# Where the sums of weight blocks are made in the seven-product groups of a decoder trunk

## The chip, the cores and the metric

The kernel runs on one NeuronCore of a Trainium2 chip. The core has a matrix engine (TensorE, PE in the profile, with its weight loads as PEld), a vector engine (VectorE, DVE), a scalar engine (ScalarE, ACT), a general engine (GpSimd, POOL), and a queue engine (SyncE, SP) that here only issues transfers. Sixteen DMA engines move data between HBM and SBUF (the on-chip memory) for all queues. TensorE writes its results to PSUM. The metric is the device time of one execution in microseconds (us); lower is better.

## What is computed

Two layers of a decoder trunk on 256 tokens of width 2048, then a final RMSNorm. Per layer:

```python
h = rms_norm(x, norm_w)
proj = h @ w_in                       # split into qa, ka, va, za, qi, ki, wi, ub, zb, qc, kc, vc, zc, gates
y_a = (dsa_attention(...) * silu(za)) @ w_a_out
y_b = (conformer_conv(ub, ...) * silu(zb)) @ w_b_out
y_c = (stick_breaking_attention(qc, kc, vc) * silu(zc)) @ w_c_out
g = sigmoid(gates).reshape(b, s, 3, 2048)
merged = g[:, :, 0] * y_a + g[:, :, 1] * y_b + g[:, :, 2] * y_c
x = x + merged @ w_out
```

All of it is float32. The change lies in the second half of a layer: the merge gates (`gates`, 6144 columns of `w_in`), the three branch projections, and `w_out`.

## The kernel before

**Split weights.** Each float32 weight unit (256 rows by 512 columns, 512 KB, held as 128x1024) is turned into two halves of a faster format: ScalarE rounds it (`high`, L247, tile `wh`), VectorE takes the rest (`low`, L251, tile `wl`, = raw minus `wh`). Three matmuls stand for one product: activation high by `wh`, activation low by `wh`, activation high by `wl`, in this order. `wh` and `wl` have three buffers each.

**Steps.** The second half of a layer is a list of steps (`Step`), run by `run` (L551). A plain step (`plain`) takes one unit for both token tiles: 12 matmuls of 512 columns. `run` works ahead: at step s it issues raw loads up to step s+7 (`PARTS` + `LOADS`), does the early events of s, converts the unit of step s+2 (`high`, `low`), then emits the matmuls of step s and its late events. Raw loads go to SP's queue, into a ring of five `raw` buffers and one buffer `va` that attention also uses (`raw_unit`, L406).

**Groups of seven products.** `Seven` (L446) computes one block of 256 tokens by 1024 columns over half of the inner dimension with seven half-size products instead of eight (M1 to M7). Each product has two half steps, a and b, of 6 matmuls. Weight blocks are called here B00, B01, B10, B11 (row half, column half). M1, M2 and M3 use B00, B10 and B11 as they are loaded. The others use sums:

| product | block sum | where it is kept |
|---|---|---|
| M5 | B01 + B00 | `ar` (`homes[h]`) |
| M6 | B01 + B00 + B11 | `ar` |
| M4 | B01 + B00 + B11 + B10 | `ar` |
| M7 | B01 + B11 | `ph` and `pl` (`third[h]`) |

Before the change they are made thus, for each half: `two` loads B01 into `ar` (SP queue); `plus` adds the raw B00 of M1 on VectorE (L473); `more` adds B11 with an accumulating DMA from GpSimd's queue (L470), after M5 has been converted; `plus` adds the raw B10 of M2 on VectorE; `three` loads B01 again into `ph` or `pl` (L478), and `and_more` adds B11 with a second accumulating DMA (L481). There are five groups per layer (four for gates, one for `w_out`), ten in all, so twenty halves. `ph` and `pl` are also working tiles of attention (`pair`).

**Order.** `gather` weaves the half steps of a group with plain steps (`y`: other chunks or branch projections; `c`, `d`: the rest of the group's own columns over the other half of the inner dimension). Per layer: a gate chunk, a branch-A projection, group g2, a projection, group h2, the 16 steps `zb`, group g1, group h1, two projections, then the `w_out` steps `qs` with group `o`. In the background VectorE works off the taps of a depthwise convolution (L678) and its normalisation (`conv_norm`), started by `norm` at an offset from the first step of `zb`; and attention's last part (`stick`) ends while g2 begins. Every branch result is turned by a way over DRAM (`turned`: transposes on VectorE, transfers L294 and L300 on GpSimd's queue).

**Queues.** Every engine runs its instructions in order. A scheduler orders them when the program is built, from priorities and its own estimate of time; a transfer without a tie to another instruction may be put well ahead of where it is written. `issue_after(ins)` ties an instruction behind `ins` on the same queue; `high_priority` moves instructions ahead.

Of the kernel before, what the change touches and what calls it, by code (L numbers as in the profile page):

```python
# [11 lines left out]
ALU = mybir.AluOpType  # L12
AX = mybir.AxisListType

P = 128
# [13 lines left out]
PARTS = 2  # L29
LOADS = 5  # L30
LATER = 10
# [20 lines left out]
def trunk(ctx: ExitStack, tc: tile.TileContext, x, w_in, xt, w_a, w_b, w_c, w_out,  # L52
          fnw, consts, out):
    nc = tc.nc
# [14 lines left out]
    def issue_after(ins):  # L69
        return nullcontext() if fixed[0] else tc.issue_after(ins)  # L70
# [45 lines left out]
    class Lazy(list):  # L116
        def __init__(self, n, make):
            super().__init__([None] * n)
            self.make = make
# [182 lines left out]
    def turned(srcs, use, later=LATER, tmp=None):  # L302


        n = len(srcs)
        if tmp is None:
            tmp = tp.tile([P, n * 512], F32, tag="zt", bufs=1, name=nm("zt"))
        c = srcs[0].shape[1]
        z = away([v.rearrange("p (k e) -> p k e", e=P) for v in srcs], tmp[:, :n * c])

        def rest():
            y = tp.tile([P, n * 512], F32, tag="zy", bufs=1, name=nm("zy"))
            y = y[:, :n * c].rearrange("p (u k i) -> p u k i", u=n * 4, i=32)
            back(z, y)
            yield later - 2
            yield from use(y)

        pending.append([count[0] + 2, rest()])
# [78 lines left out]
    def source(w, k0, kn, c0, n=512):  # L397
        return w[k0 * P:(k0 + kn) * P, c0:c0 + n].rearrange("(k p) c -> p k c", p=P)
# [3 lines left out]
        return [v[:, i] for i in range(2)]  # L402

    ring = [0]

    def raw_unit(w, k0, c0):  # L406
        ring[0] += 1
        if ring[0] % (RAWS + 1):
            raw = wp.tile([P, 2, 512], F32, tag="raw", bufs=RAWS, name=nm("raw"))
        else:  # L410
            raw = sp.tile([P, 2, 512], F32, tag="va", bufs=1, name=nm("va"))
        nc.sync.dma_start(raw, source(w, k0, 2, c0))
        return raw

    def plain(w, k0, c0, act, banks, start, stop, nk=2):
# [30 lines left out]
    class Seven:  # L446


        def __init__(self, w, c0, act, sums, added=("P1", "P4")):
            self.banks = banks = {}  # L450
            self.steps = {}

# [7 lines left out]
            def block(k, n, h):  # L460
                return source(w, k * 4 + h * 2, 2, c0 + n * 512)

            homes = [ar[:, h * 1024:(h + 1) * 1024].rearrange("p (k c) -> p k c", k=2) for h in range(2)]
            third = {}

            def two(h):
                nc.sync.dma_start(homes[h], block(0, 1, h))

            def more(h, k, n):
                nc.gpsimd.dma_start(homes[h], block(k, n, h), accum_op=ALU.add)  # L470

            def plus(h, name):
                nc.vector.tensor_add(homes[h], homes[h], self.steps[name, h].raw)  # L473

            def three(h):
                g = ("ph", "pl")[h]
                third[h] = tp.tile([P, 1024], F32, tag=g, bufs=1, name=nm(g)).rearrange("p (k c) -> p k c", k=2)
                nc.sync.dma_start(third[h], block(0, 1, h))  # L478

            def and_more(h):  # L480
                nc.gpsimd.dma_start(third[h], block(1, 1, h), accum_op=ALU.add)  # L481

            def product(name, a, k0, t, to, start, load, late=False):
                for h in range(2):
# [18 lines left out]
            product("M4", act, 4, 1, "Y", False, lambda h: homes[h], True)  # L503
            st = self.steps
            for h in range(2):
                st["M5", h].at(-PARTS - 9, partial(two, h), True)
                if "P1" in added:
                    st["M1", h].at(-PARTS + 1, partial(plus, h, "M1"), True)
                else:
                    st["M5", h].at(-PARTS - 5, partial(more, h, 0, 0), True)  # L510
                st["M5", h].at(-PARTS + 1, partial(more, h, 1, 1), True)
                if "P4" in added:
                    st["M2", h].at(-PARTS + 1, partial(plus, h, "M2"), True)
                else:
                    st["M6", h].at(-PARTS + 1, partial(more, h, 1, 0), True)
                st["M7", h].at(-PARTS - 8, partial(three, h), True)
                st["M7", h].at(-PARTS - 4, partial(and_more, h), True)
            held = once(ev)

            def copied(n, get):  # L520
# [183 lines left out]
    xn = next_x()  # L704
# [9 lines left out]
    for layer in range(DEPTH):  # L714
        w = w_in[layer]
# [699 lines left out]
        def emit_x(xc, accs, q, c0, ts):  # L1415
            n = xc.shape[-1]
            with tc.high_priority(offset=URGENT):
                for a_, t in zip(accs, ts):
                    nc.vector.tensor_add(xc[:, t, :], a_, xc[:, t, :])  # L1419
            if last:  # L1420
                sq = ev()
                for t in ts:
                    with tc.high_priority(offset=URGENT):
                        nc.scalar.activation(sq[:, :n], xc[:, t, :], AF.Square, accum_out=ssq[:, t, q:q + 1])  # L1424
                    nc.vector.tensor_mul(xfr[t][:, c0:c0 + n], xc[:, t, :], fwl[0][:, c0:c0 + n])
            else:
                x_squares([xc[:, t, :] for t in ts], ssq, q, ts)
                turned([xc[:, t, :] for t in ts], partial(x_parts_F, xn, c0 // P, nwn), LATER - (2, 2, 3, 4)[q],
                       t4() if q % 2 else None)

        def store_x(xc, c0):
# [53 lines left out]
            steps[-1].at(1, finished).at(-4, ask)  # L1485
            return steps

        def gates(b, j, added=("P1", "P4")):
            c0 = O_G + b * D + j * 512
            g = Seven(w, c0, hx, sums, added)  # L1490
            rest = [[plain(w, k0, c0 + i * 512, hx, lambda i=i: [g.bank(v) for v in ("XY", "ZW")[i]], False, k0 == KD - 2)
                     for k0 in range(KC, KD, 2)] for i in range(2)]
            for i in range(2):
                rest[i][-1].at(1, lambda i=i: keep_gate(b, j + i, [g.bank(v) for v in ("XY", "ZW")[i]]))
            return g, rest[0], rest[1]
# [21 lines left out]
            for ks in ((0, 1), (2, 3)):  # L1517
                differences([x8[:, i * 4 + ks[0]:i * 4 + ks[0] + 2, :] for i in range(2)], osums, ks)

        g2, c2, d2 = gates(2, 0)  # L1520
        h2, e2, f2 = gates(2, 2)
        g1, c1, d1 = gates(1, 0)
        h1, e1, f1 = gates(1, 2)
        y2, y1 = ([products(b, wy, j, gx) for j in range(4)] for b, wy, gx in ((2, wc, gc), (1, wb, gb)))
        zb = gate_steps(O_ZB, cv, gb, lambda: bool(stages))
        zb[0].at(-16, norm)
        y1[3][0].at(0, output_sums)
        if last:
            y1[3][1].at(0, lambda: nc.sync.dma_start(fwl[0], fnw.partition_broadcast(P)))
        o = Seven(wo, p0 * 512, mx, osums)  # L1530
        qs = {}
        for q in range(4):
            own = q in (p0, p0 + 1)
            banks = (lambda v: lambda: [o.bank(n) for n in v])("ZW" if q - p0 else "XY") if own else None
            qs[q] = output(q, banks, KC if own else 0)
        begin = "g.M1a y g.M5a y g.M1b y g.M5b y g.M6a y g.M6b y g.M2a y g.M2b y g.M7a g.M7b "
        rest = "g.M3a g.M3b d g.M4a d g.M4b c d c d c*2"
        steps = chunk_steps(w, O_G + 2 * 512, hx, KD, partial(keep_gate, 0, 2)) + products(0, w_a[layer], 2, ga)
        steps += gather(begin + rest, y=chunk_steps(w, O_G + 3 * 512, hx, KD, partial(keep_gate, 0, 3), wide_accs), g=g2, c=c2, d=d2)
# [5 lines left out]
        steps += y1[2] + y1[3]  # L1545
        c, d = 2 - p0, 3 - p0
        if last:
            steps += qs[c][:4] + qs[d] + gather(
                "g.M1a c g.M5a g.M1b c g.M5b g.M6a c g.M6b c g.M2a g.M2b g.M7 g.M3a g.M3b f g.M4a f g.M4b f*2 e*4",
                g=o, c=qs[c][4:], e=qs[p0], f=qs[p0 + 1])  # L1550
        else:
            steps += qs[c][:4] + qs[d][:4] + gather(
                "g.M1a c g.M5a c g.M1b d g.M5b d g.M6a c g.M6b c g.M2a d g.M2b d g.M7 g.M3a g.M3b e g.M4a e g.M4b e*2 f*4",
                g=o, c=qs[c][4:], d=qs[d][4:], e=qs[p0], f=qs[p0 + 1])
        extra = []
        if not last:
# [1 line left out]
        order = ExitStack()  # L1558
        pass
        pass  # L1560
        early_parts = run(steps, extra)
        fixed[0] = False
        order.close()
# [114 lines left out]
```

## Time and profile before

| | |
|---|---|
| time, median of 3 runs (lowest, highest) | 2024.99 us (2024.75, 2026.19) |
| the profiled execution's own time | 2028.66 us |
| its span in the trace | 2026.9 us |
| granted TensorE clock, mean | 0.997 |
| VectorE busy | 1671.6 us |
| ScalarE busy | 1140.9 us |
| GpSimd busy (issuing transfers) | 219.6 us |
| moved by DMA | 482.68 MB |

The page sums the busy time of each engine over one profiled execution; the views of its trace list waits by who waited for whom, groups of instructions, single stretches, and transfers with their time from issue to landing. An entry in square brackets on a line of the timeline is the idle time of that engine just before the instruction, and what ended it.

### The profile page before, as it was taken

How to read it: one execution, taken by the hardware profiler on the slowest of the kernel's cores; microseconds unless marked ns; L12 is line 12 of the kernel's file. 1: busy time of each engine (PE TensorE's matmuls, PEld its weight loads, DVE VectorE, ACT ScalarE, POOL GpSimd, SP SyncE). 2: the span in 40 equal slices, each digit the busy share in tenths (PEclk: the TensorE clock that was granted, in tenths of full speed). 3: DMA queues.
4: the chain of work that ended last, by engine and by line, in shares of the span. 5: the costliest groups of instructions: out<-in, count | busy, mean ns of one | idle time of the engine just before them, and what ended most of it. 6: DMA issues, size and time to landing. Idle time of an engine off the chain costs nothing. (4 is left out here: it accounts for less than half of the span.)

```text
span 2026.9 us, 25983 instructions
## 1 busy us (share of the span) xinstructions
PE 1996.2 (98%) x9266; PEld 1664.7 (82%) x9266; DVE 1671.6 (82%) x2227; ACT 1140.9 (56%) x1327; POOL 219.6 (11%) x324
## 2 busy tenths in 40 slices
PE   9999999999999999999999999999999999999998
PEld 8899888888878787878888988888888787878776
DVE  8667899878988979777885779988879989697777
ACT  7556555565655556555654555455666555565545
POOL 0111112100110001011110111121001000010110
PEclk9999999999999999999999999999999999999999
DMA  7798679855787777897877876788657888678974
GB/s 273 231 287 263 186 225 296 258 177 177 218 227 247 212 249 223 255 317 241 301 227 237 283 240 192 237 283 254 180 177 223 223 259 256 209 226 237 345 237 136
DMA packets 245378, 482.68 MB, mean 238 GB/s; under 512 B 17856, under 2 KB 30656, under 8 KB 245120
## 3 DMA queue, kind: packets, MB, share of 16 engines
q1 hardware_dynamic: 214208, 399.74, 61.8%
q0 software_dynamic: 29376, 78.14, 15.0%
q10 hardware_dynamic: 1664, 3.15, 0.4%
q8 instruction: 72, 1.18, 0.2%
q14 instruction: 58, 0.48, 0.1%
HBM read 448.18 MB, written 32.77 MB: 237 GB/s over the span
## 5 line engine op out<-in xcount | busy, mean ns | idle before, releaser
L262 PE MATMUL acc<-wh,s 128*128 128x512 f32 (+1 forms) x4528 | 1136.2, 390 | 14.1 <-ACT wh L247 11.4
L247 ACT CAST wh<-raw 128x1024 fp32r<-128x1024 f32 (+1 forms) x650 | 678.7, 1047 | 612.2 <-PE acc L262 430.1
L262 PEld LDWEIGHTS acc<-wh,s 128*128 128x128 f32 x4528 | 843.8, 188 | 183.6 <-ACT wh L247 14.3
L251 DVE TENSOR_TENSOR wl<-raw,wh 128x1024 fp32r<-128x1024 f32 (+1 forms) x651 | 787.1, 1213 | 196.0 <-ACT wh L247 193.5
L262 PE MATMUL acc<-wl,s 128*128 128x512 f32 (+1 forms) x2072 | 565.2, 389 | 3.5 <-DVE wl L251 2.9
L262 PEld LDWEIGHTS acc<-wl,s 128*128 128x128 f32 x2072 | 387.2, 188 | 88.7 <-DVE wl L251 11.4
L262 PE MATMUL mm<-wh,s 128*128 128x512 f32 x992 | 246.6, 390 | 2.4 <-DVE s L615 1.2
L262 PEld LDWEIGHTS mm<-wh,s 128*128 128x128 f32 x992 | 185.9, 188 | 42.6 <-ACT wh L247 1.6
L294 POOL DMA_DIRECT2D z<-zt x192 | 112.7, 603 | 953.5 <-DVE zt L291 935.6
L678 DVE SCALAR_TENSOR_TENSOR s<-yT,cst,s 128x256 f32<-128x256 f32 x480 | 212.2, 477 | 0.0
L262 PE MATMUL mm<-wl,s 128*128 128x512 f32 x496 | 133.0, 390 | 1.0 <-DVE wl L251 1.0
L247 ACT CAST wh<-ar 128x1024 fp32r<-128x1024 f32 x60 | 63.0, 1050 | 85.6 <-DMA ar<-in_w_in_dram 35.9
L262 PEld LDWEIGHTS mm<-wl,s 128*128 128x128 f32 x496 | 92.8, 188 | 21.5 <-DVE wl L251 2.4
L251 DVE TENSOR_TENSOR wl<-ar,wh 128x1024 fp32r<-128x1024 f32 x60 | 73.1, 1219 | 41.2 <-ACT wh L247 40.4
L247 ACT CAST wh<-va 128x1024 fp32r<-128x1024 f32 x52 | 54.5, 1049 | 45.7 <-PE acc L262 24.6
L251 DVE TENSOR_TENSOR wl<-va,wh 128x1024 fp32r<-128x1024 f32 x52 | 63.3, 1218 | 13.4 <-ACT wh L247 13.2
L473 DVE TENSOR_TENSOR ar<-ar,raw 128x1024 f32<-128x1024 f32 x37 | 45.0, 1219 | 34.0 <-DMA raw<-in_w_in_dram 24.4
L262 PEld LDWEIGHTS mm<-s,wl 128*128 128x128 f32 x512 | 66.9, 191 | 5.0
L300 POOL DMA_DIRECT2D zy<-z x50 | 37.0, 740 | 287.4 <-DMA z<-zt 96.0
L262 PE MATMUL mm<-s,wl 128*128 128x192 f32 x512 | 66.0, 271 | 0.0
L291 DVE STREAM_TRANSPOSE zt<-acc 128x512 f32<-128x512 f32 (+1 forms) x68 | 45.2, 679 | 3.5 <-PE acc L262 3.0
L470 POOL DMA_DIRECT2D ar<-in_w_in_dram x16 | 19.3, 1203 | 194.3 <-DVE wl L251 194.3
(273 smaller groups left out, 1226.9 us busy)
## 6 DMA issues: line engine op xcount, KB each, us to landing
raw<-in_w_in_dram SPq DMA_DIRECT2D x507, 512.0 KB, 4.5
raw<-in_w_out_dram SPq DMA_DIRECT2D x51, 512.0 KB, 5.4
zy<-z POOLq DMA_DIRECT2D x48, 512.0 KB, 5.5
z<-zt POOLq DMA_DIRECT2D x184, 128.0 KB, 4.5
raw<-in_w_a_dram SPq DMA_DIRECT2D x29, 512.0 KB, 4.2
va<-in_w_in_dram SPq DMA_DIRECT2D x28, 512.0 KB, 4.7
raw<-in_w_c_dram SPq DMA_DIRECT2D x26, 512.0 KB, 5.0
raw<-in_w_b_dram SPq DMA_DIRECT2D x26, 512.0 KB, 6.8
```

What stands on the lines that cost most here:

```text
L247: newest_parts[0] = nc.scalar.copy(u[1], u[0])
L251: newest_parts[1] = sub = nc.vector.tensor_sub(u[2], u[0], u[1].bitcast(F32))
L262: newest[0] = nc.tensor.matmul(o, lhsT, rhs, start=start, stop=stop, skip_group_check=True)
L291: nc.vector.transpose(tmp[:, t].rearrange("p b k i -> p k b i"), src.rearrange("p k (b c) -> p k b c", b=4, c=32))
L294: nc.gpsimd.dma_start(z[:, :, :, a, :].rearrange("t b c e -> c (t b) e"), tmp[a * 32:(a + 1) * 32].rearrange("c t b k i -> c (t b) (k i)"))
L300: nc.gpsimd.dma_start(y.rearrange("p (t a) k i -> p t (a k i)", a=4), z.rearrange("t b c a e -> (b c) t (a e)"))
L470: nc.gpsimd.dma_start(homes[h], block(k, n, h), accum_op=ALU.add)
L473: nc.vector.tensor_add(homes[h], homes[h], self.steps[name, h].raw)
L678: nc.vector.scalar_tensor_tensor(o, yT[:, c, q:q + S], wq, o, op0=ALU.mult, op1=ALU.add)
```

## The change

Four things are changed.

1. `three` loads B11, not B01, and `and_more` and the `more` of B11 are not used any more. VectorE makes all sums: `first_sums` (third += `ar`, giving B01 + B11, then `ar` += raw of M1, giving B01 + B00), `second_sum` (`ar` = third + raw of M1, giving B01 + B00 + B11), `last_sum` (`ar` += raw of M2). All are issued with high priority. A half thus has four VectorE additions and two plain loads, where it had two additions, two plain loads and two accumulating DMAs.
2. The loads `two` and `three` are tied behind the newest raw load in SP's queue, and stand `lead` and `lead` + 1 steps ahead of M5's conversion (7 and 8, for the first group 5 and 6); before, `two` stood 9 ahead of it and `three` 8 ahead of M7's.
3. The weaving: one plain step moves from between M5a and M1b to between M7a and M7b. In the last layer the four steps of the chunk `d` are woven into group `o` and no longer stand ahead of it.
4. `norm` starts 22 steps ahead of `zb`, not 16; the transposed parts of x are used one step earlier in two of four chunks (`LATER`); the ring of raw buffers starts anew in each layer.

```diff
     class Seven:
-        def __init__(self, w, c0, act, sums, added=("P1", "P4")):
+        def __init__(self, w, c0, act, sums, lead=7, added=("P4",)):
...
             def two(h):
-                nc.sync.dma_start(homes[h], block(0, 1, h))
+                with issue_after(last_raw[0].ins):
+                    nc.sync.dma_start(homes[h], block(0, 1, h))
...
-            def plus(h, name):
-                nc.vector.tensor_add(homes[h], homes[h], self.steps[name, h].raw)
...
-                nc.sync.dma_start(third[h], block(0, 1, h))
-
-            def and_more(h):
-                nc.gpsimd.dma_start(third[h], block(1, 1, h), accum_op=ALU.add)
+                with issue_after(last_raw[0].ins):
+                    nc.sync.dma_start(third[h], block(1, 1, h))
+
+            def first_sums(h):
+                with tc.high_priority():
+                    nc.vector.tensor_add(third[h], third[h], homes[h])
+                    nc.vector.tensor_add(homes[h], homes[h], self.steps["M1", h].raw)
+
+            def second_sum(h):
+                with tc.high_priority():
+                    nc.vector.tensor_add(homes[h], third[h], self.steps["M1", h].raw)
+
+            def last_sum(h):
+                with tc.high_priority():
+                    nc.vector.tensor_add(homes[h], homes[h], self.steps["M2", h].raw)
...
             for h in range(2):
-                st["M5", h].at(-PARTS - 9, partial(two, h), True)
-                if "P1" in added:
-                    st["M1", h].at(-PARTS + 1, partial(plus, h, "M1"), True)
-                else:
-                    st["M5", h].at(-PARTS - 5, partial(more, h, 0, 0), True)
-                st["M5", h].at(-PARTS + 1, partial(more, h, 1, 1), True)
+                st["M5", h].at(-PARTS - lead, partial(two, h), True)
+                st["M1", h].at(-PARTS, partial(first_sums, h), True)
+                st["M5", h].at(-PARTS + 1, partial(second_sum, h), True)
                 if "P4" in added:
-                    st["M2", h].at(-PARTS + 1, partial(plus, h, "M2"), True)
+                    st["M2", h].at(-PARTS + 2, partial(last_sum, h), True)
                 else:
                     st["M6", h].at(-PARTS + 1, partial(more, h, 1, 0), True)
-                st["M7", h].at(-PARTS - 8, partial(three, h), True)
-                st["M7", h].at(-PARTS - 4, partial(and_more, h), True)
+                st["M5", h].at(-PARTS - lead - 1, partial(three, h), True)
...
-        zb[0].at(-16, norm)
+        zb[0].at(-22, norm)
...
-        begin = "g.M1a y g.M5a y g.M1b y g.M5b y g.M6a y g.M6b y g.M2a y g.M2b y g.M7a g.M7b "
+        begin = "g.M1a y g.M5a g.M1b y g.M5b y g.M6a y g.M6b y g.M2a y g.M2b y g.M7a y g.M7b "
         rest = "g.M3a g.M3b d g.M4a d g.M4b c d c d c*2"
...
         if last:
-            steps += qs[c][:4] + qs[d] + gather(
-                "g.M1a c g.M5a g.M1b c g.M5b g.M6a c g.M6b c g.M2a g.M2b g.M7 g.M3a g.M3b f g.M4a f g.M4b f*2 e*4",
-                g=o, c=qs[c][4:], e=qs[p0], f=qs[p0 + 1])
+            steps += qs[c][:4] + gather(
+                "g.M1a d g.M5a g.M1b d g.M5b d g.M6a d g.M6b c g.M2a c g.M2b c g.M7a c g.M7b g.M3a g.M3b f g.M4a f g.M4b f*2 e*4",
+                g=o, c=qs[c][4:], d=qs[d], e=qs[p0], f=qs[p0 + 1])
         else:
             steps += qs[c][:4] + qs[d][:4] + gather(
-                "g.M1a c g.M5a c g.M1b d g.M5b d g.M6a c g.M6b c g.M2a d g.M2b d g.M7 g.M3a g.M3b e g.M4a e g.M4b e*2 f*4",
+                "g.M1a c g.M5a g.M1b c g.M5b d g.M6a d g.M6b c g.M2a c g.M2b d g.M7a d g.M7b g.M3a g.M3b e g.M4a e g.M4b e*2 f*4",
```

More of the change, by code (lines that the diff above doesn't have):

```diff
@@ L404, in trunk @@
     ring = [0]
+    last_raw = [None]
     def raw_unit(w, k0, c0):
@@ L411, in raw_unit @@
             raw = sp.tile([P, 2, 512], F32, tag="va", bufs=1, name=nm("va"))
-        nc.sync.dma_start(raw, source(w, k0, 2, c0))
+        last_raw[0] = nc.sync.dma_start(raw, source(w, k0, 2, c0))
         return raw
@@ L1427, in emit_x @@
                 x_squares([xc[:, t, :] for t in ts], ssq, q, ts)
-                turned([xc[:, t, :] for t in ts], partial(x_parts_F, xn, c0 // P, nwn), LATER - (2, 2, 3, 4)[q],
+                turned([xc[:, t, :] for t in ts], partial(x_parts_F, xn, c0 // P, nwn), LATER - (2, 2, 4, 5)[q],
                        t4() if q % 2 else None)
@@ L1486, in output, with gates @@
             return steps
-        def gates(b, j, added=("P1", "P4")):
+        def gates(b, j, lead=7):
             c0 = O_G + b * D + j * 512
-            g = Seven(w, c0, hx, sums, added)
+            g = Seven(w, c0, hx, sums, lead)
             rest = [[plain(w, k0, c0 + i * 512, hx, lambda i=i: [g.bank(v) for v in ("XY", "ZW")[i]], False, k0 == KD - 2)
@@ L1518, in output_sums @@
                 differences([x8[:, i * 4 + ks[0]:i * 4 + ks[0] + 2, :] for i in range(2)], osums, ks)
-        g2, c2, d2 = gates(2, 0)
+        g2, c2, d2 = gates(2, 0, 5)
         h2, e2, f2 = gates(2, 2)
@@ L1529, in trunk @@
             y1[3][1].at(0, lambda: nc.sync.dma_start(fwl[0], fnw.partition_broadcast(P)))
-        o = Seven(wo, p0 * 512, mx, osums)
+        o = Seven(wo, p0 * 512, mx, osums, added=("P4",))
         qs = {}
@@ L1560, in trunk @@
         pass
+        ring[0] = 0
         early_parts = run(steps, extra)
```

## The prediction

> **What bounds the kernel now.** I read the page first, then the list of waits of TensorE, then the timeline at each wait, then transfers, then VectorE by stretches.
>
> ```profile
> PE 1996.2 (98%) x9266; PEld 1664.7 (82%) x9266; DVE 1671.6 (82%) x2227; ACT 1140.9 (56%) x1327; POOL 219.6 (11%) x324
> ```
>
> TensorE is the bound, busy for all but 30.7 us of the span of 2026.9. Its pace, in a stretch without waits:
>
> ```profile
> 1601.61 1.77 PEld L262 LDWEIGHTS mm<-wh,s 128*128 128x128 f32 x8
> ```
>
> Eight weight loads start within 1.77 us less the 0.19 us of one, so a matmul of 512 columns starts every (1.77 - 0.19) / 7 = 0.226 us. A plain step of 12 is 2.71 us, a half step of 6 is 1.36 us. The change alters neither number nor size of the matmuls; it can only touch the waits, listed here from 10 us on (who waited for whom, us in total, times, longest):
>
> ```profile
> PE acc L262 <- ACT wh L247: 11.4, 7, 2.6
> PE acc L262 <- DVE wl L251: 2.9, 8, 1.1
> PE acc L262 <- ACT acc L522: 2.7, 1, 2.7
> PE mm L262 <- DVE s L615: 1.2, 1, 1.2
> PE mm L262 <- ACT wh L247: 1.0, 1, 1.0
> PE mm L262 <- DVE wl L251: 1.0, 2, 0.6
> PE mm L262 <- ACT s L614: 0.3, 1, 0.3
> ```
>
> That is 20.5 us. The timeline of TensorE places the large ones (the idle time stands in brackets):
>
> ```profile
> 608.45 2.08 PE L262 MATMUL acc<-wh,s 128*128 128x512 f32 x4 [2.62 <-ACT wh L247]
> ...
> 891.29 3.68 PE L262 MATMUL acc<-wh,s 128*128 128x512 f32 x8 [2.10 <-ACT wh L247]
> ...
> 1037.90 0.50 PE L262 MATMUL acc<-wh,s 128*128 128x512 f32 x1 [0.28 <-ACT wh L247]
> ...
> 1782.71 0.50 PE L262 MATMUL acc<-wl,s 128*128 128x512 f32 x1 [1.15 <-DVE wl L251]
> ...
> 1800.71 1.21 PE L262 MATMUL mm<-wl,s 128*128 128x512 f32 x4 [0.62 <-DVE wl L251]
> ...
> 1895.23 2.11 PE L262 MATMUL acc<-wh,s 128*128 128x512 f32 x8 [1.76 <-ACT wh L247]
> ```
>
> Of the first row's seven waits, 11.4 us, those at 891 and 1895 make 3.9 and that at 1037 makes 0.3; the other four, 7.2 us, lie at 608, 793, 1609 and 1796 us, each in front of a half of M6 in a gate group. The 2.7 us behind L522 lie at 1964 us, in front of M6 of the last layer's group `o`.
>
> ScalarE is only the messenger. Its own timeline just before:
>
> ```profile
> 607.36 1.04 ACT L247 CAST wh<-ar 128x1024 fp32r<-128x1024 f32 x1 [5.81 <-DMA ar<-in_w_in_dram]
> ...
> 889.25 1.04 ACT L614 CAST s<-zy 128x1024 fp32r<-128x1024 f32 x1 [6.67 <-DMA zy<-z]
> ...
> 1962.55 1.04 ACT L247 CAST wh<-ar 128x1024 fp32r<-128x1024 f32 x1 [5.91 <-DMA ar<-in_w_out_dram]
> ```
>
> At 607 and 1962 the conversion of M6 waits for the accumulating DMA into `ar`; the casts ahead of the three waits between read `ar` for M6 likewise. At 889 (and alike before 1895) ScalarE stands in front of a cast whose transposed branch result is late, with the next weight conversion queued behind it. Why transfers are late, by issue to landing (median us last):
>
> ```profile
> raw<-in_w_in_dram SPq DMA_DIRECT2D x507, 512.0 KB, 4.5
> ```
> ```profile
> ar<-in_w_in_dram POOLq DMA_DIRECT2D x16, 512.0 KB, 8.6
> ```
>
> An accumulating transfer takes twice a plain one, and M6's can be issued only once M5 is converted.
>
> **The change, part by part.** *Accumulating DMAs out.* Forty transfers of 512 KB go. The five waits for them, 7.2 + 2.7 = 9.9 us, go with them: the sum behind M5 becomes one VectorE addition. What is late next there is that addition, below. After two of the long waits, at 608 and at 891, TensorE ran on a lower clock:
>
> ```profile
> 605.00:615.00 10.00, 7.38 (x27) 5.70 (x26) 6.57 (x8) 5.04 (x5) 0.00 (x0) 0.83 0.39 118
> 687.00:719.00 32.00, 31.30 (x136) 24.91 (x135) 32.00 (x39) 16.55 (x17) 2.38 (x2) 1.00 0.91 271
> 719.00:763.00 44.00, 44.00 (x197) 36.47 (x196) 31.81 (x30) 22.74 (x26) 3.11 (x5) 1.00 0.74 230
> 763.00:825.00 62.00, 60.33 (x263) 48.70 (x263) 58.33 (x66) 39.12 (x44) 7.91 (x9) 1.00 0.83 238
> 890.00:900.00 10.00, 8.71 (x31) 7.12 (x32) 7.14 (x6) 7.16 (x9) 0.72 (x1) 0.83 1.04 361
> ```
>
> (Stretch, busy of PE, PEld, DVE, ACT, POOL, clock, DMA share, GB/s.) In the first and the last stretch the clock is 0.83, so 10 x 0.17 = 1.7 us were lost in each besides the wait. The first goes too: 1.7. The Trainium skill ("TensorE: Matmul & The Clock Gate", Part 1: The HAM clock gate) says that the clock halves after at least one idle window of about 3.4 us. By that, waits of 2.62 and 2.10 us would cost no clock, and -16 would become -13; the trace disagrees, and I go by it.
>
> *Loads tied to their place.* Group `o` of layer 0 converts its first sum at 946 us, yet its loads stand from 869 us on, together with accumulations, and the transposed result's own transfer is issued between them:
>
> ```profile
> 946.68 1.05 ACT L247 CAST wh<-ar 128x1024 fp32r<-128x1024 f32 x1 [1.67 <-PE mm L262]
> ```
> ```profile
> 869.36 0.37 SPq L478 DMA_DIRECT2D ph<-in_w_out_dram  x1
> ```
> ```profile
> 877.12 1.22 POOL L481 DMA_DIRECT2D ph<-in_w_out_dram  x1 [8.42 <-DMA ph<-in_w_out_dram]
> 877.87 1.22 POOL L300 DMA_DIRECT2D zy<-z  x1
> ```
>
> That transfer lands at 889, 11 us later. With the tie, these loads move some 50 us later, and the accumulations do not exist. The waits of 2.10 and 1.76 us and the clock after the first go: 5.6 us. The moved issues pass the raw loads between on SP's queue; they wait only for `ar`, `ph` and `pl`, free since the group before.
>
> *Start of `norm`, and the last layer's order.* At 1782.71 and 1800.71 VectorE is behind; its queue holds the end of `conv_norm` there. Six steps earlier, about 13 us of it fall into the `zb` steps, where VectorE has room (719 to 763 above: 31.81 busy of 44). Those two waits go, 1.15 + 0.62 = 1.8 us. The wait of 1.2 us for L615 is for the last transposed part in the last layer; its reader stands about 4 us later in the new order, and the cast before it no longer queues behind the accumulation: 1.2 us. *Ring and `LATER`*: nothing; a load is issued five steps ahead of its conversion either way, and if one were a step late it would cost up to 2.7 us.
>
> *Weaving.* As many steps as before. Where M7a, M7b, M3a and M3b stood in a row, 5.4 us of TensorE for four conversions of 1.22, three half steps stand now; M5a and M1b, apart before, stand together. Only short waits lie there (the 2.9 us on `wl` less 1.15 at 1782 fall on seven places), so I count nothing for it, within the 1.8 us of these.
>
> *VectorE's additions in.* One costs 1.22 us:
>
> ```profile
> L473 DVE TENSOR_TENSOR ar<-ar,raw x37: 1178/1222/1228, 576.8 to 1970.6; 128x1024 f32<-128x1024 f32 x37
> ```
> ```profile
> 576.78 2.35 DVE L473 TENSOR_TENSOR ar<-ar,raw 128x1024 f32<-128x1024 f32 x2
> ```
>
> Twice two halves in ten groups make 40 more, 48.8 us, 4.9 us per group. They lie beside the matmuls as long as the conversions are in time. The tightest step is the plain one after M1a: `second_sum` of half a and `first_sums` of half b, three additions, stand in front of M1b's conversion. From M1a's start at 0: M5a is converted at 1.0 + 1.2 = 2.2 (cast, then rest); three additions, 2.35 - 1.22 = 1.13 each back to back, end at 5.6; M1b's `wl` at 6.7. TensorE starts M1b at 1.36 + 2.71 + 1.36 = 5.4 and needs `wl` after four matmuls, at 6.3: 0.4 us late, in ten groups 4.0 us. Bounds: 0 if the scheduler puts the conversion first; 1.2 us more per group if VectorE comes to that step one instruction late, 16 us. I take 4.0, nearest to the row. In the stretch 687 to 719 VectorE has no idle time; there it can only shift taps and normalisation into `zb`, whose 44 us have 12 idle. In 763 to 825 it has 3.7 idle plus what `norm` gives up.
>
> Holding M1's raw block three steps longer costs nothing: its buffer is asked for again six loads later, M2a's, five steps ahead of need. In g2, `third` is tied to attention's end, as its load was before; nothing, bounds -1 and +3 us per layer.
>
> **Sum**: 9.9 + 1.7 + 5.6 + 1.8 + 1.2 = 20.2 us go, 4.0 come: -16 us. The profiled execution took 2028.66 us with a span of 2026.9; its own time would become 2012. The median of the runs shown is 2024.99, so the median becomes 2009.
>
> **The rivals.**
>
> *All of it, and free* (0.17). The additions find gaps, and other small waits on VectorE go as well: the 20.5 us of waits and 3.4 of clock vanish: 2001. For: VectorE is 18% idle. Against: not where groups stand.
>
> *VectorE full* (0.16). In g2, h2 and g1 of both layers the additions displace conversions: of 6 x 4.9 = 29 us half lands on TensorE, 14.6 in place of 4, net -5.5: 2019. For: 32.00 of 32 busy. Against: most of the rest there is background work.
>
> *VectorE held at the head of its queue: slower* (0.10). `first_sums` waits for two loads and a raw block, and all conversions stand behind it. Such waits exist:
>
> ```profile
> DVE ar L473 <- DMA raw<-in_w_in_dram: 24.4, 9, 3.9
> ```
>
> A conversion between plain steps has slack: two steps and eight matmuls, 7.2 us, less 1.04 for the cast and 1.22 (as L473) for the rest, so 4.9 us. Waits of 24.4 / 9 = 2.7 us cost nothing. It decides from 4.9 us on: were the tied loads as late as an accumulation, 9 us instead of 4.5, a wait would be near 7.5 us and cost 2.6, in 20 halves 52 us on paper; with only the first half of each group in plain steps, 26. Net +10: 2035. Against: without accumulations the loads should land in 5.
>
> *Waits only move* (0.07): the tied loads are now what M5 and M7 wait for, as much as before: 2025.
>
> *VectorE holds up GpSimd* (0.02). Two-input additions could delay GpSimd's issuing of the transposed results: 1.2 us each at the two late ones per layer, 5 us back: 2014. Against:
>
> ```profile
> L470 POOL DMA_DIRECT2D ar<-in_w_in_dram x16: 1179/1198/1267, 588.9 to 1851.4; - x16
> ```
>
> The spread is 0.09 us with VectorE over 80% busy, so nothing holds it. The Trainium skill ("SBUF — State Buffer", SBUF: two separate sides) describes such a lock on a shared port, for two SBUF inputs only against a GpSimd operation that reads SBUF; no run here shows it.
>
> **How the numbers follow.** Forecast 2009 (0.48). Range: from 1999, the free case with g2's -1 us in both layers, to 2022, which holds the half-full VectorE and the bound of 16 us for the additions (2021); beyond lie the slower and the unchanged case, 0.17. A change under 0.2%, 4 us, cannot be told from none. Faster: forecast, free, shared port and most of the full case, 0.80; same 0.10; slower 0.10.
>
> **What would show it.** Right: no accumulating transfer in the list of issues; no cast of `wh` from `ar` idle for a DMA; no loads of `o` before 900 us; no clock of 0.83 past 20 us; additions 80 by 1.22 us. Wrong: waits of TensorE on `wl` above 7 us in total (VectorE full), or VectorE idle for `ph`, `pl` or `ar` loads over 5 us at once (held).

## The result and the profile after

| | before | after |
|---|---|---|
| time, median of 5 runs (lowest, highest) | 2024.99 us (2023.88, 2027.38) | 2014.38 us (2012.42, 2016.85) |
| profiled execution, and its span | 2028.66, 2026.9 | 2015.98, 2014.1 |

The ratio is 0.9947, with an interval of 0.9932 to 0.9961: 10.6 us faster, where 16 were forecast. From here on TensorE's idle time counts past the first 10 us; the start is the same in all kernels.

The page of after, its busy times and its transfers:

```profile
PE 1991.2 (99%) x9266; PEld 1667.6 (83%) x9266; DVE 1715.3 (85%) x2267; ACT 1142.7 (57%) x1327; POOL 171.2 (9%) x284
...
DMA packets 234498, 461.70 MB, mean 229 GB/s; under 512 B 17216, under 2 KB 30016, under 8 KB 234240
```

The change does what it says: forty transfers of 512 KB are gone (482.68 - 461.70 = 21.0 MB), and VectorE has 40 instructions and 43.7 us more. The waits of TensorE in after (who waited for whom, us in total, times, longest):

```profile
PE mm L262 <- ACT s L620: 4.2, 1, 4.2
PE acc L262 <- DVE wl L251: 3.1, 4, 1.8
PE acc L262 <- ACT wh L247: 2.5, 4, 1.0
PE mm L262 <- ACT wh L247: 2.4, 2, 1.3
...
PE mm L262 <- DVE wl L251: 0.5, 1, 0.5
```

That is 12.7 us instead of 20.5. The row left out belongs to the start. All the large waits of before are gone, at 608, 793, 891, 1609, 1796, 1895 and 1964 us, and so are the two at 1782 and 1800. In their place stand others. The timeline of TensorE in after:

```profile
590.93 1.45 PE L262 MATMUL acc<-wh,s 128*128 128x512 f32 x5 [1.00 <-ACT wh L247]
...
772.93 1.07 PE L262 MATMUL acc<-wh,s 128*128 128x512 f32 x4
774.73 0.73 PE L262 MATMUL acc<-wl,s 128*128 128x512 f32 x2 [0.73 <-DVE wl L251]
775.29 2.00 PE L262 MATMUL mm<-wh,s 128*128 128x512 f32 x8
...
1770.25 0.74 PE L262 MATMUL acc<-wl,s 128*128 128x512 f32 x2 [0.45 <-DVE wl L251]
...
1926.06 0.73 PE L262 MATMUL acc<-wl,s 128*128 128x512 f32 x2 [1.79 <-DVE wl L251]
...
1957.04 2.07 PE L262 MATMUL mm<-wh,s 128*128 128x512 f32 x4 [4.24 <-ACT s L620]
```

Four kinds are to be seen. **M1b**: at 774 and 1770 M1b waits for `wl` after its four matmuls with `wh`, 1.18 us in all. In the second layer the same half step of the same group waited in before too, 1.15 us at 1782; there only 0.45 are left. **M5a of the last `o`**: at 1926 TensorE waits 1.79 us for the `wl` that is made from `ar`. **The first group, g2**: at 590.93 (and for 0.95 us at 1586) M5a waits for its cast. **The last branch**: at 1957 TensorE waits 4.24 us for a turned result, and the weight casts have nothing to do with it.

The rows at 773 also show what a wait costs beyond its bracket. Four matmuls at 0.226 us make the next one due at 773.83; it came at 774.73, 0.90 late, where the bracket says 0.73. The one behind the two `wl` matmuls was due at 775.18 and came at 775.29. So this wait took 0.28 us more than its bracket; the sums below take that for each.

What VectorE did ahead of 590.93, and ScalarE's cast of M5a:

```profile
583.96 1.22 DVE L482 TENSOR_TENSOR ph<-ph,ar 128x1024 f32<-128x1024 f32 x1
585.10 1.22 DVE L251 TENSOR_TENSOR wl<-raw,wh 128x1024 fp32r<-128x1024 f32 x1
586.23 1.22 DVE L482 TENSOR_TENSOR pl<-pl,ar 128x1024 f32<-128x1024 f32 x1
587.36 1.22 DVE L251 TENSOR_TENSOR wl<-raw,wh 128x1024 fp32r<-128x1024 f32 x1
588.50 2.36 DVE L483 TENSOR_TENSOR ar<-ar,raw 128x1024 f32<-128x1024 f32 x2
```
```profile
589.83 1.04 ACT L247 CAST wh<-ar 128x1024 fp32r<-128x1024 f32 x1 [4.19 <-DVE ar L483]
```

The addition that M5a needs, the first of L483, is placed behind the `pl` sum of the other half, which is not needed before that half's sum for M6b.

The chain behind 1957, and ahead of it the `wl` of M5a that ends the wait at 1926, in the timelines of VectorE, GpSimd and ScalarE of after (L1386 and L1387 merge a branch result, L291 transposes it, L300 brings it back from DRAM):

```profile
1920.17 1.23 DVE L482 TENSOR_TENSOR pl<-pl,ar 128x1024 f32<-128x1024 f32 x1 [0.58 <-DMA ar<-in_w_out_dram]
...
1924.79 1.21 DVE L251 TENSOR_TENSOR wl<-ar,wh 128x1024 fp32r<-128x1024 f32 x1
...
1926.52 1.21 DVE L487 TENSOR_TENSOR ar<-ph,raw 128x1024 f32<-128x1024 f32 x1
...
1931.06 0.68 DVE L1387 TENSOR_TENSOR s<-s,t 128x512 f32<-128x512 f32 x1
1931.66 1.21 DVE L487 TENSOR_TENSOR ar<-pl,raw 128x1024 f32<-128x1024 f32 x1
...
1936.40 1.22 DVE L491 TENSOR_TENSOR ar<-ar,raw 128x1024 f32<-128x1024 f32 x1
...
1939.81 0.70 DVE L291 STREAM_TRANSPOSE zt<-s 128x512 f32<-128x512 f32 x1
```
```profile
1948.25 0.72 POOL L300 DMA_DIRECT2D zy<-z  x1 [5.11 <-ACT wh L247]
```
```profile
1955.94 1.04 ACT L620 CAST s<-zy 128x1024 fp32r<-128x1024 f32 x1 [3.87 <-DMA zy<-z]
```

The merge ends at 1931.7, but the transpose of the second token tile comes 8 us later, behind additions and conversions (the first tile's ran at 1923.06). In before both transposes ran from 1932.89 on, in one piece; what held the part up there came later, when its transfer back waited 13.47 us, in the end for L615, which was still reading the part before it out of the one buffer `zy`:

```profile
1932.89 1.29 DVE L291 STREAM_TRANSPOSE zt<-s 128x512 f32<-128x512 f32 x2
```
```profile
1950.28 0.72 POOL L300 DMA_DIRECT2D zy<-z  x1 [13.47 <-DVE s L615]
```

### The profile page after: what moved, and what is told of

Read it like the earlier page. It is cut to its first block, busy times and chain, and to the rows that moved or that the text cites. A ratio compares the mean times of both kernels' runs of the same rounds, so it can differ in the third digit from the quotient of the medians.

```text
span 2014.1 us, 25976 instructions
## 1 busy us (share of the span) xinstructions
PE 1991.2 (99%) x9266; PEld 1667.6 (83%) x9266; DVE 1715.3 (85%) x2267; ACT 1142.7 (57%) x1327; POOL 171.2 (9%) x284
## 2 busy tenths in 40 slices
DMA packets 234498, 461.70 MB, mean 229 GB/s; under 512 B 17216, under 2 KB 30016, under 8 KB 234240
## 3 DMA queue, kind: packets, MB, share of 16 engines
q8 instruction: 72, 1.18, 0.2%
## 4 chain that ended last, share of the span: by engine, by line
PE 94%; DMA 2%; DVE 2%; issue 1%; ACT 0%; POOL 0%; DVEq 0%; SPq 0%; POOLq 0%; ACTq 0%
PE acc L262 74%; PE mm L262 17%; DMA ar<-in_w_out_dram 1%; DVE wl L251 1%; DMA va<-in_w_a_dram 1%; PE mm L1099 1%; PE mm L1189 0%; DMA zy<-z 0%; DVE ar L483 0%; PE mm L1292 0%; PE mm L1157 0%; PE mm L1239 0%; ACT wh L247 0%; DMA z<-zt 0%; PE mm L866 0%
## 5 line engine op out<-in xcount | busy, mean ns | idle before, releaser
L262 PEld LDWEIGHTS mm<-wl,s 128*128 128x128 f32 x496 | 93.6, 189 | 20.5 <-DVE wl L251 0.9
L300 POOL DMA_DIRECT2D zy<-z x50 | 35.9, 719 | 298.3 <-DMA z<-zt 104.5
L291 DVE STREAM_TRANSPOSE zt<-acc 128x512 f32<-128x512 f32 (+1 forms) x68 | 45.4, 681 | 3.6 <-PE acc L262 3.0
L620 ACT CAST s<-zy 128x1024 fp32r<-128x1024 f32 x20 | 20.9, 1046 | 13.6 <-DVE zy L670 9.8
L621 DVE TENSOR_TENSOR s<-zy,s 128x1024 fp32r<-128x1024 f32 x20 | 24.4, 1221 | 3.7 <-ACT s L620 3.7
```

Source lines behind the costliest of these rows:

```text
L262: newest[0] = nc.tensor.matmul(o, lhsT, rhs, start=start, stop=stop, skip_group_check=True)
L291: nc.vector.transpose(tmp[:, t].rearrange("p b k i -> p k b i"), src.rearrange("p k (b c) -> p k b c", b=4, c=32))
L300: nc.gpsimd.dma_start(y.rearrange("p (t a) k i -> p t (a k i)", a=4), z.rearrange("t b c a e -> (b c) t (a e)"))
L620: nc.scalar.copy(h, src)
L621: nc.vector.tensor_sub(l, src, h.bitcast(F32))
```

## The experiments

Each experiment ran beside the kernel before, in one of three sessions and in four to twelve runs; ratios are to the before of the same session, with intervals of 95%.

| kernel | median us | ratio (interval) |
|---|---|---|
| after | 2014.38 | 0.9947 (0.9932 to 0.9961) |
| e3 before + sums on VectorE only | 2007.82 | 0.9922 (0.9904 to 0.9941) |
| e4 before + ties only | 2043.77 | 1.0099 (1.0082 to 1.0117) |
| e7 after, additions left out | 1997.87 | 0.9859 (0.9844 to 0.9875) |
| e6 after + 20 more VectorE operations | 2022.91 | 0.9981 (0.9968 to 0.9993) |
| e1 after, last merge and transposes first | 2006.54 | 0.9915 (0.9899 to 0.9932) |
| e2 after, old order of the last layer | 2014.04 | 0.9950 (0.9933 to 0.9966) |
| e8 after without ties | 2007.08 | 0.9907 (0.9892 to 0.9922) |
| e14 after, `o` alone without ties | 2004.62 | 0.9895 (0.9882 to 0.9909) |
| e15 e14, M5a's sum first in g2 | 2002.86 | 0.9888 (0.9874 to 0.9902) |
| e13 e8, norm's small operations and M5a's sum first | 2007.47 | 0.9910 (0.9896 to 0.9924) |
| e9 e3, `norm` at -22 | 2006.50 | 0.9902 (0.9887 to 0.9918) |
| e5 after, `norm` at -16 | 2013.29 | 0.9941 (0.9927 to 0.9955) |

### The sums alone, and the ties alone

e3 takes over the sums, with their loads at the new places in the list of steps, and leaves weaving, `norm`, `LATER` and the ring as they were, without ties (as a diff from after):

```diff
-                with issue_after(last_raw[0].ins):
-                    nc.sync.dma_start(homes[h], block(0, 1, h))
+                nc.sync.dma_start(homes[h], block(0, 1, h))
...
-                with issue_after(last_raw[0].ins):
-                    nc.sync.dma_start(third[h], block(1, 1, h))
+                nc.sync.dma_start(third[h], block(1, 1, h))
...
-        zb[0].at(-22, norm)
+        zb[0].at(-16, norm)
...
```

> The kernel before with the sums on VectorE alone: four additions per half and no accumulating transfers, loads at their new offsets but not tied to the raw loads; old weaving, old start of the normalisation, old use of the transposed parts, old ring. By the prediction's terms this has the 9.9 + 1.7 us of the accumulation waits less 4.0 us for the additions, so 2025 - 7.6 = 2017. If most of the gain hangs on the ties and the weaving, it stays within 3 us of 2025. If the ties and the weaving are worth nothing by themselves, it is at 2014 like the changed kernel, or below, as the last layer's old order has no wait of 4.2 us.

e4 is before with the two ties:

```diff
...
-                nc.sync.dma_start(homes[h], block(0, 1, h))
+                with issue_after(last_raw[0].ins):
+                    nc.sync.dma_start(homes[h], block(0, 1, h))
...
-                nc.sync.dma_start(third[h], block(0, 1, h))
+                with issue_after(last_raw[0].ins):
+                    nc.sync.dma_start(third[h], block(0, 1, h))
```

> The kernel before with one edit: the plain loads of the block sums (into ar, ph and pl) are tied behind the newest raw load in SP's queue; the accumulating transfers stay. By the prediction the burst of group o's loads near 870 to 890 us and near 1880 us goes, with the waits of 2.1 and 1.8 us and the low clock after the first: 5.6 us, so 2019. The rival (the burst was late because of the accumulations in it, not because it stood early): no more than 1 us, 2024.

The sums alone gain more than the whole change: 2007.82, the last of the outcomes named for them, in which the ties and the weaving are worth nothing by themselves. The two intervals overlap a little, but the slowest run of e3 (2011.57) was faster than the fastest of after (2012.42). The ties alone lose 18 us, which neither expectation had. The waits of TensorE in e4, and two casts of M6 on ScalarE:

```profile
PE acc L262 <- ACT wh L247: 18.8, 7, 6.5
PE acc L262 <- ACT acc L525: 12.2, 1, 12.2
```
```profile
609.11 1.04 ACT L247 CAST wh<-ar 128x1024 fp32r<-128x1024 f32 x1 [11.11 <-DMA ar<-in_w_in_dram]
...
1979.55 1.04 ACT L247 CAST wh<-ar 128x1024 fp32r<-128x1024 f32 x1 [15.40 <-DMA ar<-in_w_out_dram]
```

The waits at 891 and 1895 are gone, as expected of the tie, but those for accumulations grew from 9.9 to some 30 us, and the mean granted clock fell from 0.997 to 0.990. GpSimd's timeline in e4 shows why:

```profile
1963.51 1.23 POOL L484 DMA_DIRECT2D ph<-in_w_out_dram  x1 [4.99 <-DMA ph<-in_w_out_dram]
1968.08 1.21 POOL L484 DMA_DIRECT2D pl<-in_w_out_dram  x1 [3.34 <-DMA pl<-in_w_out_dram]
1968.82 2.90 POOL L472 DMA_DIRECT2D ar<-in_w_out_dram  x2
```

GpSimd now has to wait for the later loads of `ph` and `pl`, and M6's accumulations into `ar` stand behind them in its queue; in before, they were issued at 1953.15 and 1958.34 (by then TensorE stands some 7.5 us later in e4). e3 has no tie, and neither wait (891, 1895). So either is enough: with the tie the burst at `o` goes even with its accumulations, and without accumulations it does no harm in its early place.

### What the additions cost

e7 leaves the 80 additions out, so that it computes less; loads, casts and matmuls stay:

```diff
             def first_sums(h):
-                with tc.high_priority():
-                    nc.vector.tensor_add(third[h], third[h], homes[h])
-                    nc.vector.tensor_add(homes[h], homes[h], self.steps["M1", h].raw)
+                pass
...
```

> The changed kernel without any addition of block sums: M4 to M7 use single blocks in place of the sums, so this leaves out part of the computation; loads, conversions and matmuls are all there. It prices the 80 additions. Prediction: they cost 4.0 us, plus whatever displaced work costs; with the 6.6 us near 1957 us now known to come from displaced merges, the time is 2004. If the additions were wholly hidden but for that wait, 2008. If VectorE is full, 2000 or less.

e6 adds one operation of the same size to each half:

```diff
                     nc.vector.tensor_add(homes[h], third[h], self.steps["M1", h].raw)
+                    nc.vector.tensor_tensor(homes[h], homes[h], homes[h], op=ALU.max)
```

> The changed kernel with one more VectorE operation of the same size per half, on the block sum right behind second_sum (the maximum of the sum with itself, which changes no value): 20 operations of 1.22 us in all, 24 us of VectorE. If an addition costs what the prediction took, 4.0 us for 40, about 2 us more: 2016. If VectorE is full around the groups, most of it lands on TensorE: 2025 to 2035. If additions are free, 2014.

All waits of TensorE that are left in e7, the start's among them:

```profile
PE mm L262 <- ACT wh L247: 1.3, 2, 0.7
PE mm L862 <- DVE eps L79: 1.1, 1, 1.1
PE acc L262 <- ACT wh L247: 0.5, 2, 0.3
```

So the 80 additions cost after 2014.38 - 1997.87 = 16.5 us (17.8 by the ratios), and without them 27 us of before are gone. Of the outcomes named for e7 this is the one for a full VectorE, 2000 or less. Forty of the 80 stood in before too, so the 16.5 bounds the price of the 40 new ones from above; but the waits at 590, 774, 1586, 1926 and 1957, most of it, are not in before. Both numbers fit the waits. From e7 to after, idle time grows from 1.8 to 12.7, 10.9; eight more waits at 0.28 make 2.2; and low clock at 1957 (below) makes 3.0: 16.1. In e6, twenty operations more cost 8.5 us (6.9 by the ratios), 0.43 each: a third of their 1.22 us lands on TensorE, though VectorE was 15% idle. That lies between the 2016 and the 2025 named beforehand. Not all of it is a full queue: two of e6's new waits, 1.51 and 1.44 us at 601 and 1600, are for M6a's cast, directly behind the added operation.

### The wait at 1957

e1 moves the merge and the transposes ahead of the additions:

```diff
-            merge(b, j, y, [sg[:, t, :] for t in range(NT)])
-            if b == 1:
-                turned([mg(j, t) for t in range(NT)], partial(use_m, j), LATER - 3 * (j == 3))
+            with tc.high_priority(offset=URGENT) if last and b == 1 and j == 3 else nullcontext():
+                merge(b, j, y, [sg[:, t, :] for t in range(NT)])
+                if b == 1:
+                    turned([mg(j, t) for t in range(NT)], partial(use_m, j), LATER - 3 * (j == 3))
```

> The changed kernel, with one edit in the last layer: the gated merge and the transposes of the last quarter of branch B (j = 3) are given the highest priority, ahead of the additions of group o. In the changed kernel TensorE waits 4.2 us near 1957 us for the split of the last transposed part and then runs at half pace for some 2.4 us. Theory A (the new additions push the merge and the second transpose back on VectorE, from 1933 us to 1940 us, and so the part arrives late): the wait goes, the clock stays up, and the time falls by 5 to 7 us, to 2008 us. Theory B (the transposed part is late because its own transfers over DRAM are slow among the raw loads): the transposes come earlier, but the wait stays above 3 us and the time stays within 2 us of 2014.

e2 gives the last layer its old weaving:

```diff
-            steps += qs[c][:4] + gather(
-                "g.M1a d g.M5a g.M1b d g.M5b d g.M6a d g.M6b c g.M2a c g.M2b c g.M7a c g.M7b g.M3a g.M3b f g.M4a f g.M4b f*2 e*4",
-                g=o, c=qs[c][4:], d=qs[d], e=qs[p0], f=qs[p0 + 1])
+            steps += qs[c][:4] + qs[d] + gather(
+                "g.M1a c g.M5a g.M1b c g.M5b g.M6a c g.M6b c g.M2a g.M2b g.M7 g.M3a g.M3b f g.M4a f g.M4b f*2 e*4",
+                g=o, c=qs[c][4:], e=qs[p0], f=qs[p0 + 1])
```

> The changed kernel with the last layer's old weaving (four steps of chunk d ahead of group o, as before the change). Theory A (group o comes four steps earlier in the new order, so that its additions meet the merges of the last branch): the merges run undisturbed, the wait of 4.2 us falls under 1.5 us, and the time falls by 3 to 6 us, to 2008 to 2011. Theory B (slow transfers): the reader of the late part stands 4 us earlier in this order, so the wait grows to some 8 us and the time rises to 2018.

e1 took the wait away and 7.8 us with it: the 4.24, its 0.28, and 3.0 of low clock are 7.5. There the transposes run at 1917.86 and 1922.12, and the transfer back is issued at 1935.15. So the late merge and transpose are the cause. e2 took the wait away as well, but not the time: waits on `wl` rose to

```profile
PE acc L262 <- DVE wl L251: 5.5, 6, 1.8
...
PE mm L262 <- DVE wl L251: 1.2, 1, 1.2
```

Neither theory had that: VectorE's load in `o` is too dense under either order, and the order only chooses who is late. What makes it dense, e8 and e14 tell. e8 takes all ties out of after (the diff of e3's first lines), e14 only those of `o`:

```diff
-        def __init__(self, w, c0, act, sums, lead=7, added=("P4",)):
+        def __init__(self, w, c0, act, sums, lead=7, added=("P4",), tie=True):
...
-                with issue_after(last_raw[0].ins):
+                with issue_after(last_raw[0].ins) if tie else nullcontext():
...
-        o = Seven(wo, p0 * 512, mx, osums, added=("P4",))
+        o = Seven(wo, p0 * 512, mx, osums, added=("P4",), tie=False)
```

> The changed kernel, with the loads of the block sums not tied to the raw loads; weaving, start of the normalisation and all else as in the change. The sums alone, untied and in the old weaving, ran at 2008, the change at 2014. Theory A (the tie costs: loads that could have come early come late, and the additions bunch up in front of the merges): 2007 to 2010, and TensorE's waits at the start of g2 (1.3 and 1.0 us per layer) and in group o shrink. Theory B (the new weaving of the last layer costs by itself, whatever the loads do): the wait of 4.2 us near 1957 us stays, 2013 to 2015.

> The changed kernel, with the loads of group o alone not tied; the eight gate groups keep the tie. Theory (the tie costs in group o, where the late loads push the additions into the merges of the last branch): the wait of 4.2 us near 1957 us and those of 0.5 and 1.8 us on wl near 937 and 1926 us go, and no wait near 714 us on the normalisation's own split appears as in the kernel without any tie: 2004 to 2007. Rival (the tie costs in every group a little): 2010 to 2013.

e14 gains 9.8 us. VectorE and GpSimd in e14:

```profile
1921.29 0.71 DVE L291 STREAM_TRANSPOSE zt<-s 128x512 f32<-128x512 f32 x1
```
```profile
1931.89 0.72 POOL L300 DMA_DIRECT2D zy<-z  x1 [7.26 <-DVE s L621]
```

The transpose comes 18.5 us earlier and its transfer back 16.4. The sums of `third`, which after makes at 1909 and 1920 because their loads land then, are long done in e14:

```profile
1870.11 1.23 DVE L482 TENSOR_TENSOR ph<-ph,ar 128x1024 f32<-128x1024 f32 x1 [2.83 <-DMA ar<-in_w_out_dram]
...
1874.13 1.22 DVE L482 TENSOR_TENSOR pl<-pl,ar 128x1024 f32<-128x1024 f32 x1
```

So two additions less stand in the dense stretch. In layer 0 the tie shows in after as a stop at the head of VectorE's queue:

```profile
927.73 1.23 DVE L482 TENSOR_TENSOR ph<-ph,ar 128x1024 f32<-128x1024 f32 x1 [4.92 <-DMA ar<-in_w_out_dram]
```

Without any tie (e8) the gain is smaller, 7.3 us, though the intervals of e8 and e14 overlap: the additions of g1 now fall where `norm` splits its values for TensorE, and TensorE waits there instead:

```profile
713.95 0.39 PE L1315 MATMUL mm<-ev,ones_r 128*128 128x256 f32 x1 [1.33 <-ACT ev L1309]
```

So the early load helps at `o`, and in g1 it puts the additions beside something urgent.

### The small parts

e5 puts `norm` back to -16 in after, e9 puts it to -22 in e3:

> The changed kernel with the normalisation started 16 steps ahead as before, not 22. The prediction gave the early start 1.8 us: 2016, with waits on wl near 1775 to 1800 us back. In the sums-only kernel the early start gave nothing that could be told from none (2007.8 and 2006.5). If it is worth nothing here too, 2014.

> The sums on VectorE alone (untied, old weaving), with the normalisation started 22 steps ahead, not 16. The sums alone show TensorE waiting 1.2 us for the normalisation's own split near 719 and 1712 us and short waits on wl near 698 and 1690, some 2.2 us of lost time per layer. If the early start gives VectorE the room that the prediction claims for it (1.8 us), these go and the time falls by 2 to 4.5 us, to 2003.5 to 2006. If it only moves the load, it stays at 2008.

Both differences, 1.1 and 1.3 us and of opposite sign, are within the intervals: `norm`'s start is worth nothing that could be measured. By themselves intervals of some 3 us to either side could not exclude the forecast 1.8, but the waits at 1782 and 1800 are absent from e5 too, so the early start is not what removed them; one of 0.52 us stands in front of another half step, at 1776. In e9 TensorE waits no less for `norm`'s split: 1.57 and 0.59 us at 716 and 718, where e3 has 1.24 at 719.

e13 tries to mend e8's wait with priority for `norm`'s last operations, and takes M5a's sum ahead of the other half's `third` in g2; e15 does only the latter, on e14:

```diff
                     nc.vector.tensor_add(third[h], third[h], homes[h])
+                with tc.high_priority(offset=URGENT) if lead == 5 else tc.high_priority():
                     nc.vector.tensor_add(homes[h], homes[h], self.steps["M1", h].raw)
```

> The changed kernel with no tie at all, the same order in g2, and the small additions and splits of the normalisation's two sums at high priority. The kernel without ties (2007) waits 2.1 us per layer near 714 us for those splits, as the additions of g1 are made there, 60 us ahead of their use. Theory (VectorE's order again): these waits go, 4.2 us, and the two of g2, 1.3 to 2.4 us: 2001 to 2003. Rival (VectorE is full there whatever the order): the wait turns into one on wl, and the time stays at 2005 to 2008.

> As the kernel with group o alone untied, and in group g2 of both layers the sum for M5a (ar + raw) goes ahead of the other half's addition into pl. In the change VectorE does four additions and two conversions in the order ph, pl, ar, ar before M5a's cast, and TensorE waits 1.0 us at 590.9 and at 1586.7 us. Theory (order on VectorE, 1.1 us of it): both waits go, and with the short ones behind them 2.4 us: 2.4 us below the kernel with o untied. Rival (the loads of ph and pl are late, the order does not matter): no difference.

e13 gained nothing: of two waits on `norm`'s split, 1.33 and 0.47 us at 714 and 716 in e8, it made one of 1.77 at 711. e15 is 1.8 us below e14, which is within the intervals. In g2 the wait for M5a's cast went (0.95 us in e14), and 0.75 and 0.16 on `wl` stand in its place. Of the 2.1 us of idle time that e15 has less, most lies elsewhere: e14 waits 0.96 and 1.21 us for M1b at 773 and 1767, and e15 does not, though the edit does not touch that group. VectorE's order in e15, in which the sum for M5a (L484) comes ahead of `pl`:

```profile
584.95 1.22 DVE L484 TENSOR_TENSOR ar<-ar,raw 128x1024 f32<-128x1024 f32 x1
586.08 1.22 DVE L482 TENSOR_TENSOR pl<-pl,ar 128x1024 f32<-128x1024 f32 x1
```

Its 2002.86 us is the lowest of all, 11.5 below after. What is left of the price of all additions there is 2002.86 - 1997.87 = 5.0 us.

## Why the prediction was half right

**Accumulating transfers out: right.** The five waits, 9.9 us, and the low clock at 608, 1.7, are gone, and e3 shows that the sums alone do it. What went as a whole was under-counted, 20.2 against 27.1 (with all 80 additions left out, so part of the 27.1 may be the price of the old forty): the forecast took the brackets alone and not the 0.28 us behind each of 17 waits (21 in before, 4 in e7; 4.8), and it left out small waits on `wl`, 2.0 us.

**Loads tied to their place: the gain was real, but the tie was not needed for it, and its price was left out.** The tie does what was said, as e4 shows. But with the accumulations gone the 5.6 us come without a tie at `o` as well (e3 and e14), so in the change it earns nothing. It was counted as free; it costs 9.8 us at `o`. The forecast's working asked only whether a moved issue would be held up in SP's queue. It did not ask what a later landing does to the reader: the first sum of VectorE then stands with its successors in one bunch. The rival "held at the head of its queue" had this mechanism; its idle times, 4.92 us at most, stayed at the slack of 4.9 that it named, and the cost arose behind it, in the work that the bunch displaced.

**VectorE's additions: the step that failed.** 4.0 forecast; the waits that after has and before had not, at 590, 774, 1586, 1770, 1926 and 1957, come to about 14 (M1b 1.7, M5a at 1926 2.1, g2 2.5, the last branch 7.5, each with what lies behind the bracket), and e7 gives 16.5 for old and new additions together. The place that was worked out, M1b's `wl`, is there, but in two groups instead of ten, at 1.7 us instead of 4.0, and for one of the two the wait is older than the change. At 774 only one addition (L487) and one transpose stand between the two conversions on VectorE, not three additions. Missing were the 7.5 us at 1957, the 2.1 at 1926, and the first group, 2.5 in both layers (its bound of +3 per layer held). "VectorE full" named a half of the additions' time as the share that lands on TensorE; e6 measured a third of each operation more. But it looked for displaced conversions in g2, h2 and g1, and the dearest thing displaced was a merge with its transpose, in `o`.

**The total.** It came out at 27.1 - 16.5 = 10.6, where 20.2 - 4.0 = 16.2 was forecast. Gains and price were both taken too small, by 6.9 and by 12.5, and that the sum is off by only 5.6 is partly luck.

**The last layer's order: the sign was wrong.** The reader of the last turned part did wait 1.2 us in before, at 1968, behind a wait of 2.7 for an accumulation. The forecast counted on the new order and on the end of that wait to bring 1.2 us. It did not ask when the part itself would come: TensorE comes to its reader 13 us sooner (at 1966.05 - 0.26 in before, at 1957.04 - 4.24 in after), while the transfer of the part is issued only 2 us sooner (1950.28 and 1948.25), held up now by the displaced transpose. The end of the wait alone does not bring this about: in e3 it is gone too, the transfer is issued at 1931.55, and nothing waits for the part. The order by itself is worth nothing that could be told (e2).

**`norm`**: 1.8 forecast, nothing measurable (e5, e9). Its two waits did go, with the rest of the change.

**The signs given beforehand.** No accumulating transfer is left in the list of issues, no cast of `wh` from `ar` waits for a transfer, no load of `o` comes before 900, and the additions are 80 of 1.22 us: right. Waits on `wl` are 3.6 us, under the 7 set for "VectorE full", so that sign missed the case: the displaced work did not show as `wl`. "No clock of 0.83 past 20 us" failed; TensorE ran at half its clock at 1957.

**Left open.** In g2 of both layers TensorE still waits up to 1.3 us for a block in `va` at 582 and 1578, which attention holds; a buffer of its own was not tried. Nor was it tried which of the gate groups want the tie.

## What to carry to other kernels

An operation added with high priority has to be priced by what it displaces, up to that work's own reader, not by the conversion next to it; on a VectorE that was busy for 85%, 80 additions cost a sixth of their length (16.5 of 97.6 us), and 20 operations more a third. When waits are removed, TensorE comes to every later reader sooner: ask of each chain that feeds one whether it comes sooner by as much (here 2 us against 13). A load that is put just in time can bunch the work that reads it, as it did in `o`. And each part of a change is worth a run of its own: here the sums alone did better than the sums with all that came along.

## What the hardware showed

The granted clock did not follow the length of a wait alone. Three waits, each with the matmuls behind it, of after, of e6 and of before:

```profile
1957.00:1962.00 5.00, 4.96 (x12) 3.91 (x13) 2.36 (x2) 1.23 (x2) 0.00 (x0) 0.50 0.06 22
```
```profile
1932.98 0.77 PE L262 MATMUL acc<-wl,s 128*128 128x512 f32 x2 [2.11 <-DVE wl L251]
1933.58 3.65 PE L262 MATMUL mm<-wh,s 128*128 128x512 f32 x8
```
```profile
1964.13 1.20 PE L262 MATMUL acc<-wh,s 128*128 128x512 f32 x4 [2.70 <-ACT acc L522]
```

In the first, a stretch of 5 us (columns as in the stretches above), the clock is 0.50 after the wait of 4.24 us; some 14 matmuls take 0.43 us instead of 0.226, so about 3.0 us are lost on top of the wait. In the second, a wait of 2.11 us is followed by eight matmuls in 3.65 us, where 2.00 is usual. In the third, a longer wait, 2.70, is followed by four at the full pace, 1.20. The Trainium skill ("TensorE: Matmul & The Clock Gate", Part 1: The HAM clock gate) says that activity is counted over a window of about 3.4 us that runs freely. That would let the place of a wait in the window decide, and the traces bear it out, although the clock is halved after idle times well below that window. In each of the 14 traces the changes of the granted clock lie whole multiples of 3.41 us apart. On that grid, the stretches at the waits of 2.10 us (at 891) and of 2.70 us (at 1964) in before are (same columns):

```profile
887.90:891.31 3.41, 1.31 (x7) 0.77 (x5) 0.99 (x1) 2.06 (x3) 0.00 (x0) 1.00 1.09 272
891.31:894.73 3.42, 3.42 (x8) 2.74 (x9) 2.94 (x4) 2.77 (x3) 0.00 (x0) 0.50 1.04 383
1959.70:1963.11 3.41, 1.73 (x8) 1.11 (x6) 0.00 (x0) 0.56 (x1) 0.00 (x0) 1.00 1.10 294
1963.11:1966.53 3.42, 2.14 (x8) 1.49 (x9) 2.87 (x3) 3.30 (x5) 0.00 (x0) 1.00 0.60 110
```

The wait of 2.10 us falls into one stretch whole, leaves TensorE idle for 2.10 of its 3.41 us, and the next stretch runs at half the clock. The wait of 2.70 us is cut in two by the grid, with 1.7 and 1.3 us idle in the two stretches, and the clock stays up. Counted over the stretches at full clock in all 14 traces, each of the 26 with 1.90 us or more of idle time is followed by one at half the clock, and none of the 8132 with 1.82 us or less is. What happens between these two values no trace shows.
